# ScalarE takes the first MLP's eviction, and block inverses and reads from DRAM get places in the weight stream

## The chip, the cores and the metric

One core of a Trainium2 chip runs the whole program. The metric is the device time of one execution in microseconds (us), the median of several runs. TensorE (PE) multiplies, VectorE (DVE) and ScalarE (ACT) do element-wise work, and SyncE (SP) issues the DMAs, in order, one queue. Every engine works through its own list of instructions in order.

## The reference, cut to what matters

Two blocks in a chain, on 256 tokens (272 with 16 meta tokens in the first block's mixer) of width 2048, all in float32. The first has attention, an S5 state space mixer and a squared-ReLU MLP; the second has three branches (Hyena, HGRN2, gated DeltaNet) and an MLP of its own. The lines that the change touches:

```python
def first_block(...):
    ...
    h2 = _rmsnorm(h_res, norm_mlp_g[l])
    h_res = h_res + jnp.square(jax.nn.relu(h2 @ w_up[l])) @ w_down[l]     # 2048 -> 8192 -> 2048

def _delta_scan(q, k, v, g, beta, s0):          # once on the context, once on x, both directions
    ...
    a = eye + jnp.where(strict, jnp.einsum('bhtk,bhsk->bhts', kb, kc) * decay, 0.0)
    sol = lax.linalg.triangular_solve(a, rhs, left_side=True, lower=True, unit_diagonal=False)
    ...

def forget(fz, lb):                              # HGRN2: log forget gate lf and key kk
    f = lb + (1.0 - lb) * jax.nn.sigmoid(fz)
    return heads(jnp.log(jnp.maximum(f, HG_F_MIN))), heads((1.0 - lb) * jax.nn.sigmoid(-fz))
```

The context runs through DeltaNet and HGRN2 too, for their states alone. `mod_c` and `mod` (adaLN) are products of a vector with `w_ada`.

## The kernel before, in words

**The stream.** 1016 pieces of weights, 128 x 1024 floats (512 KB) each, go one by one through the same steps (`load_w`, L326): SP issues the DMA into `w` (4 buffers), ACT copies it rounded to `wh` (L334), DVE subtracts what is left over into `wl` (L335; 3 buffers each), and PE makes three products from it, with the input split the same way: wh·xh, wh·xl (or wl·xh) and wl·xh. `linear` (L355 to L357) has the weights move past 128 tokens at a time, 512 columns wide; `linear_t` (L390 to L392) has the weights stand and 256 tokens move past. This text counts places in the stream by pieces.

**Accumulators.** PSUM has three of them (tag `a`). A pass of `linear_t` uses two and has 8 matmuls of each kind to a piece, first all for one accumulator, then all for the other.

**The first MLP** (`mlp`, L977) takes pieces 153 to 408: four groups of 32 pieces up (8 passes of 4) and 32 down. Each pass up gives two tiles `ps` (128 x 256). DVE evicts one with max(ps, 0)·rstd in one instruction (L988, recorded as L541, the helper `stt`) into `r` (2 buffers), ACT squares it (L989), ACT copies it rounded (L402) and DVE subtracts (L403): the input of the way down. The second MLP, on pieces near the end, has no rstd to multiply by, and ACT evicts there (L986).

**Work beside the stream.** The order of everything is set when the program is built, by a scheduler that takes instructions by priority bands: stores to and loads from DRAM by the helper `dma` first, then what belongs to a weight piece, then other work, then the products. `tc.issue_after(ins)` holds an instruction back until behind `ins` on the same engine; it is an order, not a semaphore. Beside the first MLP run `ada_steps` (L436: one 128 x 1024 product with the vector `cb` on DVE, L460, for every few pieces), then `delta_context` (L1378: two halves of 4 heads) and `gla_context`. From piece 409 on the second block's input products are spilled to DRAM in the order dk, dq, dv, ab, dz, hq, ff, fb, hi, hg, hy (`spill_t`, `spill_i`), and `delta_x`, `gla_x` and the Hyena branch read them back and work beside the stream.

**DeltaNet** (`delta_heads`, L1252 on): `conv_silu` (L1105) reads a spilled tile and makes a short convolution; `l2n` (L1118) squares it on ACT (L1124) and sums over channels on PE (L1125); `delta_gates` (L1137) has four small transposes (L1161); `block_inverse` (L1182) inverts 32 x 32 triangles, 31 steps of a product (L1201, recorded as L538, tile `T4c`) and a sum (L1202, `T4a`) on DVE, of t x t elements at step t; then PE merges blocks.

**HGRN2** (`gla_x`): DVE and ACT make the log gates `E` and keys `qE` for 4 heads, SP writes them to DRAM (`xlf` L1507, `xkk` L1508) and reads them back for each head (recorded as L250, the helper `dma`, into `Bh`), and PE turns each head's log gates (L1529).

Of the kernel before, what the change touches and what calls it, by code (L numbers as in the profile page):

```python
# [208 lines left out]
def emit(tc, I, out, vat, cat):  # L209
# [169 lines left out]
    def linear_t(xh, xl, W, ci, n, evict, mid=None):  # L379
# [4 lines left out]
        for kb in range(nkb):  # L384
            for i, h, l in load_w(W[ci, kb]):
                for c in range(2):
                    for j in range(4):
                        k = kb * 8 + i * 4 + j
                        s = slice(j * 256 + c * 128, j * 256 + (c + 1) * 128)
                        T.matmul(acc[c], h[:, s], xh[k][:, 0:n], start=(k == 0), stop=False)  # L390
                        T.matmul(acc[c], h[:, s], xl[k][:, 0:n], start=False, stop=False)  # L391
                        T.matmul(acc[c], l[:, s], xh[k][:, 0:n], start=False, stop=(k == nk - 1))  # L392
# [43 lines left out]
    def ada_steps(p, row, dst, j0, n):  # L436
# [371 lines left out]
    def spill_ab(xT, dst):  # L808
        ps = psum("a", [32, NT])
        with band(0):  # L810
# [5 lines left out]
            tt(l[:, :512], w[:, :512], h[:, :512].bitcast(F32), ALU.subtract)  # L816
        with band(2):
            for k in range(16):
                sl = slice(k * 32, k * 32 + 32)
                T.matmul(ps, h[:, sl], xT[0][k][:, 0:NT], start=(k == 0), stop=False)  # L820
# [182 lines left out]
    wa_p[0] = es_wa.enter_context(tc.tile_pool(name="wa", bufs=2))  # L1003
    ride(ada_steps(ada_p, 0, mod, 32, 48), RATES[0])
# [100 lines left out]
    def conv_silu(p, o, src, r0, wname, wcol, row):  # L1105
# [4 lines left out]
        ts(o, a, w[1], ALU.mult)  # L1110
# [7 lines left out]
    def l2n(p, pk, xs, scales):  # L1118
# [18 lines left out]
    def delta_gates(p, pk, src):  # L1137
# [22 lines left out]
        for c in range(2):  # L1160
            T.transpose(ps[:, c, 0], e[:, c * 128:(c + 1) * 128], ident[:32, :32])  # L1161
            T.transpose(ps[:, c, 1], be[:, c * 128:(c + 1) * 128], ident[:32, :32])
# [19 lines left out]
    def block_inverse(p, MX, XT, KD):  # L1182
# [69 lines left out]
    def delta_heads(p, pk, src, h0, nh, gates, row, S_in, S_out, tb):  # L1252
# [5 lines left out]
        kT = [conv_silu(pk, tb([128, NT], f"kT{j}"), src["dk"], (j0 + j) * 128, "dck", j0 + j, row) for j in range(nk)]  # L1258
        qT = [conv_silu(pk, tb([128, NT], f"qT{j}"), src["dq"], (j0 + j) * 128, "dcq", j0 + j, row)
              for j in range(nk if full else 0)]  # L1260
        l2n(p, pk, kT + qT, [1.0] * nk + [128.0 ** -0.5] * len(qT))
# [52 lines left out]
        block_inverse(p, MX, XT, KD)  # L1314
# [63 lines left out]
    def delta_context():  # L1378
# [11 lines left out]
        for half in range(2):  # L1390
            delta_heads(p, p2_, cd, half * 4, 4, gates, NT, None, S0d, tb)
# [12 lines left out]
    xd["hi"] = scratch("xhi", [NT, 1024])  # L1404
    spill_t("w2_dk", uT, xd["dk"], mid=lambda: turn_u(3))
# [51 lines left out]
    def delta_x():  # L1457
# [3 lines left out]
        gates = delta_gates(eg.enter_context(tc.tile_pool(name="dg", bufs=1)), dk_p, xd["ab"])  # L1461
# [16 lines left out]
        o, last = delta_heads(p, p2_, xd, 0, 8, gates, 64, S0d, None, tb)  # L1478
# [5 lines left out]
    def gla_x():  # L1484
# [29 lines left out]
        for h in range(8):  # L1514
# [7 lines left out]
            for d in range(2):  # L1522
# [5 lines left out]
                for t in range(2):  # L1528
                    T.transpose(ps[:, t], lf[:, t * 128:(t + 1) * 128], ident)  # L1529
# [430 lines left out]
```

## Time and profile before

| | before |
|---|---|
| runs, median of 3 | 3569.97 us |
| lowest and highest run | 3565.4 and 3572.29 us |
| profiled execution, its own time | 3558.18 us |
| its span | 3556.4 us |
| granted TensorE clock, mean | 0.986 |
| DVE busy | 2472.0 us (70%) |
| ACT busy | 1868.0 us (53%) |

The span is the stretch from the first to the last instruction that the profile shows, 1.8 us shorter than that execution's own time. Busy shares are means over the whole program; a stage of 80 us with a full engine can't be seen in them. "A <- B: total, times, longest" in the view of waits means that an instruction of A stood idle until B was done.

### The profile page before, as it was taken

The page shows a single profiled execution, that of the slowest core. Times are in us where ns is not written, and L with a number is a line of the kernel's source. Part 1 is how long each engine was busy: PE and PEld are TensorE (multiplying, and loading weights), DVE is VectorE, ACT ScalarE, POOL GpSimd, SP SyncE. Part 2 cuts the span into 40 slices and gives each one's busy share as a digit, 9 for nine tenths or more (in the row PEclk, how much of TensorE's full clock was granted, in tenths as well). Part 3 has the DMA queues.
Part 4 walks back from the last instruction along what each step waited for, and adds up shares of the span by engine and source line. Part 5 has one row for each costly group of instructions (what it writes and reads, how often), then busy time and mean ns, then how long its engine had stood idle before and what let it go on. Part 6 is the DMA issues. An engine that isn't in the chain of part 4 may idle for free.

```text
span 3556.4 us, 60034 instructions
## 1 busy us (share of the span) xinstructions
PE 3454.9 (97%) x23748; PEld 2981.6 (84%) x23748; DVE 2472.0 (70%) x3806; ACT 1868.0 (53%) x2936; POOL 2.6 (0%) x13
## 2 busy tenths in 40 slices
PE   7999999999999999999999999999999999999998
PEld 5567899887888989888898889887887798989897
DVE  6778756696968767656946898848855755555557
ACT  5568746545456534445456666545444454545453
POOL 0000000000000000000000000000000000000000
PEclk9999999999999999999999999999999999999999
DMA  7754465665667888765648645565566567666655
GB/s 243 263 183 128 150 216 190 185 206 180 216 204 261 273 287 279 249 203 156 190 125 265 191 123 164 173 189 171 168 191 211 180 220 226 218 220 223 213 191 173
DMA packets 262772, 719.94 MB, mean 202 GB/s; under 512 B 51229, under 2 KB 96453, under 8 KB 261445
## 3 DMA queue, kind: packets, MB, share of 16 engines
q1 hardware_dynamic: 262490, 716.10, 62.9%
q8 instruction: 186, 3.05, 0.3%
q14 instruction: 96, 0.79, 0.1%
HBM read 684.98 MB, written 31.01 MB: 201 GB/s over the span
## 4 chain that ended last, share of the span: by engine, by line
PE 48%; DVE 4%; DMA 2%; ACT 1%; issue 1%; SPq 0%; DVEq 0%; ACTq 0%
PE ps L357 8%; PE ps L356 8%; PE ps L355 8%; PE ps L392 6%; PE ps L391 6%; PE ps L390 6%; DVE wl L335 1%; ACT wh L334 1%; PE ps L1547 0%; DMA xlf<-E 0%; DVE T4c L538 0%; PE ps L1586 0%; PE ps L1709 0%; PE ps L1654 0%; PE ps L1599 0%
## 5 line engine op out<-in xcount | busy, mean ns | idle before, releaser
L335 DVE TENSOR_TENSOR wl<-w,wh 128x1024 fp32r<-128x1024 f32 x1016 | 1239.1, 1221 | 760.7 <-ACT wh L334 756.8
L334 ACT ACTIVATE wh<-w 128x1024 fp32r<-128x1024 f32 x1016 | 1075.2, 1059 | 1129.0 <-PE ps L357 619.7
L390 PE MATMUL ps<-Ah,wh 128*128 128x256 f32 (+1 forms) x3904 | 1110.5, 285 | 15.1 <-DVE r L541 10.0
L392 PE MATMUL ps<-Ah,wl 128*128 128x256 f32 (+1 forms) x3904 | 1115.9, 286 | 9.4 <-DVE wl L335 9.2
L391 PE MATMUL ps<-Al,wh 128*128 128x256 f32 (+1 forms) x3904 | 1112.6, 285 | 0.0
L390 PEld LDWEIGHTS ps<-Ah,wh 128*128 128x128 f32 x3904 | 741.8, 190 | 30.4 <-DVE r L541 12.2
L392 PEld LDWEIGHTS ps<-Ah,wl 128*128 128x128 f32 x3904 | 741.7, 190 | 25.6 <-DVE wl L335 12.6
L391 PEld LDWEIGHTS ps<-Al,wh 128*128 128x128 f32 x3904 | 738.4, 189 | 9.4 <-issue 7.5
L357 PE MATMUL ps<-wh,Bl 128*128 128x512 f32 x1344 | 534.1, 397 | 0.0
L356 PE MATMUL ps<-wl,Bh 128*128 128x512 f32 x1344 | 528.9, 394 | 2.5 <-DVE wl L335 2.5
L355 PE MATMUL ps<-wh,Bh 128*128 128x512 f32 x1344 | 529.4, 394 | 1.3 <-DVE r L541 1.0
L356 PEld LDWEIGHTS ps<-wl,Bh 128*128 128x128 f32 x1344 | 252.8, 188 | 63.9 <-DVE wl L335 5.3
L356 PE MATMUL ps<-wl,Ah 128*128 128x512 f32 x752 | 301.2, 400 | 0.0
L355 PE MATMUL ps<-wh,Ah 128*128 128x512 f32 x752 | 299.8, 399 | 0.4 <-ACT stg L1797 0.4
L357 PE MATMUL ps<-wh,Al 128*128 128x512 f32 x752 | 299.8, 399 | 0.0
L355 PEld LDWEIGHTS ps<-wh,Bh 128*128 128x128 f32 x1344 | 253.2, 188 | 55.1 <-DVE r L541 1.4
L357 PEld LDWEIGHTS ps<-wh,Bl 128*128 128x128 f32 x1344 | 252.5, 188 | 55.1 <-issue 0.8
L356 PEld LDWEIGHTS ps<-wl,Ah 128*128 128x128 f32 x752 | 140.4, 187 | 38.4 <-issue 7.4
L357 PEld LDWEIGHTS ps<-wh,Al 128*128 128x128 f32 x752 | 140.5, 187 | 36.5 <-issue 5.4
L355 PEld LDWEIGHTS ps<-wh,Ah 128*128 128x128 f32 x752 | 140.6, 187 | 35.7 <-issue 3.7
L460 DVE SCALAR_TENSOR_TENSOR wa<-wa,cb 128x1024 f32<-128x1024 f32 x96 | 116.9, 1217 | 5.0 <-ACT cb L446 5.0
L989 ACT ACTIVATE r<-r 128x256 f32<-128x256 f32 x128 | 53.0, 415 | 75.7 <-DVE r L541 73.7
(581 smaller groups left out, 3374.2 us busy)
## 6 DMA issues: line engine op xcount, KB each, us to landing
w<-in_w_ff_dram SPq DMA_DIRECT2D x288, 512.0 KB, 4.8
w<-in_w_up_dram SPq DMA_DIRECT2D x128, 512.0 KB, 5.2
w<-in_w_down_dram SPq DMA_DIRECT2D x128, 512.0 KB, 5.2
w<-in_w_ada_dram SPq DMA_DIRECT2D x96, 512.0 KB, 4.6
wa<-in_w_ada_dram SPq DMA_DIRECT2D x96, 512.0 KB, 5.8
w<-in_w_gate_dram SPq DMA_DIRECT2D x96, 512.0 KB, 4.2
w<-in_w_out_dram SPq DMA_DIRECT2D x64, 512.0 KB, 4.3
w<-in_w_hy_dram SPq DMA_DIRECT2D x48, 512.0 KB, 4.3
```

The costliest lines, as they stand in the source:

```text
L334: A.activation(out=h, in_=w, func=AF.Copy)
L335: pace[1] = V.tensor_tensor(out=l, in0=w, in1=h.bitcast(F32), op=ALU.subtract)
L355: T.matmul(acc[t], xh[k][:, lo:hi], hs, start=(k == 0), stop=False)
L356: T.matmul(acc[t], xh[k][:, lo:hi], ls, start=False, stop=False)
L357: T.matmul(acc[t], xl[k][:, lo:hi], hs, start=False, stop=(k == nk - 1))
L390: T.matmul(acc[c], h[:, s], xh[k][:, 0:n], start=(k == 0), stop=False)
L391: T.matmul(acc[c], h[:, s], xl[k][:, 0:n], start=False, stop=False)
L392: T.matmul(acc[c], l[:, s], xh[k][:, 0:n], start=False, stop=(k == nk - 1))
L460: V.scalar_tensor_tensor(out=w, in0=w, scalar=1.0, in1=cb, op0=ALU.mult, op1=ALU.mult, accum_out=part[:, j, i:i + 1])
L989: A.activation(out=r, in_=r, func=AF.Square)
```

## The change

1. **Eviction.** In the first MLP ACT now takes max(ps, 0) out of PSUM and DVE multiplies the result in SBUF by rstd (`tt(r, r, scale)`); square, copy and subtraction follow as they did. That is 64 ACT instructions more; DVE has 64 multiplications in place of 64 evictions.
2. **Block inverses.** A `Pacer` holds each of the 62 operations of a block inverse behind the subtraction `wl` of a given weight piece: it starts at piece k, gives each piece a budget, and an operation of step t costs 60 + t². The context's halves begin at pieces m0 + 15 and m0 + 85 with budget 800 (m0 = 153, the first MLP's start), that of x at m1 + 62 with 1250 (m1 = 409, the start of the spills).
3. **Work on x that reads DRAM.** The first operation of eight `conv_silu` is held behind the subtractions of pieces m1 + 9 to m1 + 22, the matmuls of `l2n` behind the first product of piece m1 + 23, the gates' transposes behind that of m1 + 46, and the log gates' transposes of the first HGRN2 head behind that of m1 + 108.
4. **Second `cb`.** In `ada_steps` the second half of the vector is loaded three pieces ahead of its use.

Nothing else is added or taken away; PE, DVE and SP have as many instructions of each kind as before, but for the 64 of point 1.

```diff
+    subs, prods = [], []
+    class Pacer:
+        def __init__(self, k, per):
+            self.k, self.per, self.left = k, per, per
+        def __call__(self, cost):
+            if self.left < cost and self.left < self.per:
+                self.k, self.left = self.k + 1, self.per
+            self.left -= cost
+            return tc.issue_after(subs[min(self.k, len(subs) - 1)].ins)
...
                 pace[1] = V.tensor_tensor(out=l, in0=w, in1=h.bitcast(F32), op=ALU.subtract)
+                subs.append(pace[1])
...
             for j in range(2):
...
-                T.matmul(acc[t], xh[k][:, lo:hi], hs, start=(k == 0), stop=False)
+                mm = T.matmul(acc[t], xh[k][:, lo:hi], hs, start=(k == 0), stop=False)
+                if t == 0 and j == 0:
+                    prods.append(mm)
...
         for at, (i, j) in enumerate(steps):
+            own = wa_p[0] is not None
             if j == 0:
+                if i and own:
+                    yield
                 cb = tl(p, [128, 1024], "cb")
-                nc.sync.dma_start(cb, I["cvec"][row, i * 1024:(i + 1) * 1024].partition_broadcast(128))
+                with ExitStack() as es:
+                    if i and own:
+                        es.enter_context(tc.issue_after(pace[0].ins))
+                    nc.sync.dma_start(cb, I["cvec"][row, i * 1024:(i + 1) * 1024].partition_broadcast(128))
                 A.activation(out=cb, in_=cb, func=AF.Silu)
-            own = wa_p[0] is not None
+                if i and own:
+                    yield
+                    yield
...
             def ev(j, ps):
                 r = tl(mw_p, [128, NT], "r")
-                if scale is None:
-                    A.activation(out=r, in_=ps, func=AF.Relu)
-                else:
-                    stt(r, ps, 0.0, scale, ALU.max, ALU.mult)
+                A.activation(out=r, in_=ps, func=AF.Relu)
+                if scale is not None:
+                    tt(r, r, scale, ALU.mult)
                 A.activation(out=r, in_=r, func=AF.Square)
...
+    def place(seq, k):
+        return ExitStack() if k is None else tc.issue_after(seq[k].ins)
...
-        ts(o, a, w[1], ALU.mult)
+        with place(subs, at):
+            ts(o, a, w[1], ALU.mult)
...
-            T.matmul(ps, C("onecol", 7 - j, 7 - j + n), sq, start=(j == 0), stop=(j == n - 1))
+            with place(prods, at):
+                T.matmul(ps, C("onecol", 7 - j, 7 - j + n), sq, start=(j == 0), stop=(j == n - 1))
...
         for t in range(1, 32):
-            tt(tm[:, 0:t, 0:t], X[:, 0:t, 0:t], U[:, 0:t, t].unsqueeze(1).to_broadcast([P, t, t]), ALU.mult)
-            V.tensor_reduce(out=X[:, 0:t, t], in_=tm[:, 0:t, 0:t], axis=AX.X, op=ALU.add, negate=True)
+            with pacer(60 + t * t):
+                tt(tm[:, 0:t, 0:t], X[:, 0:t, 0:t], U[:, 0:t, t].unsqueeze(1).to_broadcast([P, t, t]), ALU.mult)
+            with pacer(60 + t * t):
+                V.tensor_reduce(out=X[:, 0:t, t], in_=tm[:, 0:t, 0:t], axis=AX.X, op=ALU.add, negate=True)
...
-            delta_heads(p, p2_, cd, half * 4, 4, gates, NT, None, S0d, tb)
+            delta_heads(p, p2_, cd, half * 4, 4, gates, NT, None, S0d, tb, Pacer(m0 + 15 + 70 * half, 800))
...
-        o, last = delta_heads(p, p2_, xd, 0, 8, gates, 64, S0d, None, tb)
+        o, last = delta_heads(p, p2_, xd, 0, 8, gates, 64, S0d, None, tb, Pacer(m1 + 62, 1250), m1)
...
-                for t in range(2):
-                    T.transpose(ps[:, t], lf[:, t * 128:(t + 1) * 128], ident)
+                with place(prods, m1 + 108 if h == 0 else None):
+                    for t in range(2):
+                        T.transpose(ps[:, t], lf[:, t * 128:(t + 1) * 128], ident)
```

**DVE in the first MLP**, steps 27 to 29 of the context's first block inverse (`T4c`, `T4a`: the inverse; `wl`: the stream; `r`: the eviction or its product; `Bl`: the hidden tile's subtraction; `wa`: adaLN; `x`: a product of the way down being added). Before:

```order
L538 TENSOR_TENSOR T4c_14446<-T4a_14445,T4b_14444 64x27x27
L1202 TENSOR_REDUCE T4a_14445<-T4c_14446 64x27
L541 SCALAR_TENSOR_TENSOR r_8048<-ps_7923,rsb_7051 128x256
L335 TENSOR_TENSOR wl_8097<-w_8094,wh_8096 128x1024
L403 TENSOR_TENSOR Bl_8052<-r_8048,Bh_8051 128x256
L541 SCALAR_TENSOR_TENSOR r_8055<-ps_7924,rsb_7051 128x256
L460 SCALAR_TENSOR_TENSOR wa_7931,adap_7233<-wa_7931,cb_7234 128x1024
L403 TENSOR_TENSOR Bl_8059<-r_8055,Bh_8058 128x256
L335 TENSOR_TENSOR wl_8130<-w_8127,wh_8129 128x1024
L538 TENSOR_TENSOR T4c_14446<-T4a_14445,T4b_14444 64x28x28
L335 TENSOR_TENSOR wl_8160<-w_8157,wh_8159 128x1024
L1202 TENSOR_REDUCE T4a_14445<-T4c_14446 64x28
```

With the change, steps 27 and 28:

```order
L565 TENSOR_TENSOR T4c_14510<-T4a_14509,T4b_14508 64x27x27
L1241 TENSOR_REDUCE T4a_14509<-T4c_14510 64x27
L348 TENSOR_TENSOR wl_8430<-w_8427,wh_8429 128x1024
L565 TENSOR_TENSOR T4c_14510<-T4a_14509,T4b_14508 64x28x28
L348 TENSOR_TENSOR wl_8448<-w_8445,wh_8447 128x1024
L487 SCALAR_TENSOR_TENSOR wa_8348,adap_7235<-wa_8348,cb_7236 128x1024
L1241 TENSOR_REDUCE T4a_14509<-T4c_14510 64x28
L348 TENSOR_TENSOR wl_8469<-w_8466,wh_8468 128x1024
```

The first inverse, at pieces 166 to 191 before, is at 169 to 207; the second, 210 to 240 before, at 240 to 278. One of the last steps has two pieces to itself now. The first two ways up are pieces 153 to 184 and 217 to 248, the ways down 185 to 216 and 249 to 280. The inverse for x, 469 to 487 before, is at 472 to 497.

**The same engine, an eviction's product** under the first inverse, with the change (its ACT part stands at the place in the stream where DVE's eviction stood):

```order
L348 TENSOR_TENSOR wl_7973<-w_7970,wh_7972 128x1024
L565 TENSOR_TENSOR r_7919<-r_7919,rsb_7051 128x256
L565 TENSOR_TENSOR T4c_14510<-T4a_14509,T4b_14508 64x19x19
L348 TENSOR_TENSOR wl_8003<-w_8000,wh_8002 128x1024
L421 TENSOR_TENSOR Bl_7924<-r_7919,Bh_7923 128x256
L565 TENSOR_TENSOR r_7927<-r_7927,rsb_7051 128x256
```

The product stands right behind a `wl`, and one step of the inverse behind it.

**SP, where `gla_x` writes its gates and reads the first heads back** (`E` and `qE`: log gates and keys; `Bh`: a head read back; `xfb`, `xhi`: spills). Before:

```order
L1508 DMA xkk_22395<-qE_22404 128x4x256
L796 DMA xfb_15536<-stg_18695 128x256
L331 DMA w_18793<-in_w_hi_dram 128x1024
L250 DMA Bh_22499<-xkk_22395 128x256
L250 DMA Bh_22787<-xkk_22395 128x256
L796 DMA xfb_15536<-stg_18698 128x256
L331 DMA w_18811<-in_w_hi_dram 128x1024
L1507 DMA xlf_22393<-E_22403 128x4x256
L331 DMA w_18823<-in_w_hi_dram 128x1024
L331 DMA w_18855<-in_w_hi_dram 128x1024
L250 DMA Bh_22498<-xlf_22393 128x256
```

With the change:

```order
L1549 DMA xlf_22457<-E_22467 128x4x256
L344 DMA w_19161<-in_w_hg_dram 128x1024
L1550 DMA xkk_22459<-qE_22468 128x4x256
L250 DMA Bh_22562<-xlf_22457 128x256
L250 DMA Bh_22850<-xlf_22457 128x256
L832 DMA xhi_15604<-stg_19063 128x512
L250 DMA Bh_22563<-xkk_22459 128x256
L250 DMA Bh_22851<-xkk_22459 128x256
L832 DMA xhi_15604<-stg_19066 128x512
L344 DMA w_19199<-in_w_hg_dram 128x1024
```

The log gates go out and come back first now, and stand 12 pieces later in the stream; the keys follow. PE's transposes of them stand 11 to 12 pieces later, those of the other direction 17. The matmuls of `l2n` for x stand 4 to 5 pieces later on PE, the gates' transposes 4, the merge and the states of `delta_x` 11. Hyena's first two chunks stand 13 to 17 pieces later, its third and fourth where they stood.

## Rows read from the trace of the kernel before

**Rows 1.** The page's first part: busy time, share of the span, instructions.

```profile
PE 3454.9 (97%) x23748; PEld 2981.6 (84%) x23748; DVE 2472.0 (70%) x3806; ACT 1868.0 (53%) x2936; POOL 2.6 (0%) x13
```

**Rows 2.** Waits of PE, whole span: what for, us in total, times, longest.

```profile
PE ps L1529 <- DMA Bh<-xlf: 5.1, 1, 5.1
PE ps L1125 <- ACT cin L1124: 4.5, 1, 4.5
...
PE ps L1547 <- ACT seg L1513: 1.8, 1, 1.8
```

**Rows 3.** Waits of PE, 690 to 1550 us (the first MLP).

```profile
PE ps L390 <- DVE r L541: 10.0, 9, 1.7
PE ps L356 <- DVE wl L335: 1.7, 4, 0.6
...
PE ps L392 <- DVE wl L335: 1.4, 3, 0.7
```

**Rows 4.** Waits of PE, 1550 to 1580 us (the first row), 1716 to 1786 us (the second).

```profile
PE ps L392 <- DVE wl L335: 1.5, 1, 1.5
...
PE ps L392 <- DVE wl L335: 5.8, 8, 1.6
```

**Rows 5.** Stretches: length, busy PE PEld DVE ACT POOL (count), clock, DMA share, GB/s.

```profile
717.00:801.00 84.00, 78.36 (x594) 73.85 (x593) 82.62 (x127) 37.72 (x55) 0.00 (x0) 1.00 0.62 205
897.00:990.00 93.00, 87.03 (x665) 82.37 (x664) 89.84 (x125) 38.79 (x53) 0.00 (x0) 1.00 0.67 208
1350.00:1400.00 50.00, 50.00 (x425) 50.00 (x424) 37.34 (x53) 24.23 (x34) 0.00 (x0) 1.00 0.88 274
...
1567.00:1574.00 7.00, 4.49 (x14) 2.34 (x15) 4.07 (x7) 2.28 (x6) 0.00 (x0) 0.51 0.54 170
1716.00:1786.00 70.00, 64.20 (x521) 61.81 (x520) 67.87 (x95) 29.67 (x41) 0.00 (x0) 1.00 0.64 200
1918.00:1926.00 8.00, 6.37 (x17) 5.17 (x18) 2.89 (x6) 3.13 (x5) 0.00 (x0) 0.57 0.95 310
```

**Rows 6.** Tile T4c on DVE, 717 to 801 us: count, ns min/median/max, first and last start.

```profile
L538 DVE TENSOR_TENSOR T4c<-T4a,T4b x31: 145/625/1966, 721.0 to 796.6; 64x1 f32<-64x1 f32 x1, 64x4 f32<-64x4 f32 x1, 64x9 f32<-64x9 f32 x1, 64x16 f32<-64x16 f32 x1
```

**Rows 7.** Groups by line and form: busy, mean ns | idle before, ended by.

```profile
L335 DVE TENSOR_TENSOR wl<-w,wh 128x1024 fp32r<-128x1024 f32 x1016 | 1239.1, 1221 | 760.7 <-ACT wh L334 756.8 <-PE ps L392 0.9 <-issue 0.2
...
L334 ACT ACTIVATE wh<-w 128x1024 fp32r<-128x1024 f32 x1016 | 1075.2, 1059 | 1129.0 <-PE ps L357 619.7 <-PE ps L391 414.3 <-issue 32.1
...
L460 DVE SCALAR_TENSOR_TENSOR wa<-wa,cb 128x1024 f32<-128x1024 f32 x96 | 116.9, 1217 | 5.0 <-ACT cb L446 5.0
L989 ACT ACTIVATE r<-r 128x256 f32<-128x256 f32 x128 | 53.0, 415 | 75.7 <-DVE r L541 73.7
...
L541 DVE SCALAR_TENSOR_TENSOR r<-ps,rsb 128x256 f32<-128x256 f32 x64 | 26.6, 416 | 4.8 <-PE ps L392 4.8
L986 ACT ACTIVATE r<-ps 128x256 f32<-128x256 f32 x64 | 23.9, 373 | 14.3 <-PE ps L392 14.3
```

**Rows 8.** The chain that ended last, 1550 to 1580 us: start, us, what.

```profile
1558.82 2.40 DMA xdq<-stg
...
1561.24 5.05 DMA cin<-xdq
```

**Rows 9.** The same chain, 1895 to 1925 us.

```profile
1899.05 9.26 DMA xkk<-qE
...
1910.35 6.31 DMA xlf<-E
...
1916.72 2.78 DMA Bh<-xlf
```

**Rows 10.** DVE's instructions in order of time, 1895 to 1925 us.

```profile
1904.24 2.36 DVE L538 TENSOR_TENSOR E<-E,x 128x1024 f32<-128x1024 f32 x2
```

**Rows 11.** Busy time on tile T4c alone (columns of rows 5), the two operations of an inverse.

```profile
720.90:800.80 79.90, 39.50 (x62) 1.00 0.63 208
...
1721.00:1781.20 60.20, 39.90 (x62) 1.00 0.63 202
```

More of the change, by code (lines that the diff above doesn't have):

```diff
@@ L389, in linear_t @@
                         s = slice(j * 256 + c * 128, j * 256 + (c + 1) * 128)
-                        T.matmul(acc[c], h[:, s], xh[k][:, 0:n], start=(k == 0), stop=False)
+                        mm = T.matmul(acc[c], h[:, s], xh[k][:, 0:n], start=(k == 0), stop=False)
+                        if c == 0 and j == 0:
+                            prods.append(mm)
                         T.matmul(acc[c], h[:, s], xl[k][:, 0:n], start=False, stop=False)
@@ L815, in spill_ab @@
             A.activation(out=h[:, :512], in_=w[:, :512], func=AF.Copy)
-            tt(l[:, :512], w[:, :512], h[:, :512].bitcast(F32), ALU.subtract)
+            subs.append(V.tensor_tensor(out=l[:, :512], in0=w[:, :512], in1=h[:, :512].bitcast(F32),
+                                        op=ALU.subtract))
         with band(2):
@@ L819, in spill_ab @@
                 sl = slice(k * 32, k * 32 + 32)
-                T.matmul(ps, h[:, sl], xT[0][k][:, 0:NT], start=(k == 0), stop=False)
+                mm = T.matmul(ps, h[:, sl], xT[0][k][:, 0:NT], start=(k == 0), stop=False)
+                if k == 0:
+                    prods.append(mm)
                 T.matmul(ps, h[:, sl], xT[1][k][:, 0:NT], start=False, stop=False)
@@ L1003, in emit @@
     wa_p[0] = es_wa.enter_context(tc.tile_pool(name="wa", bufs=2))
+    m0 = len(subs)
     ride(ada_steps(ada_p, 0, mod, 32, 48), RATES[0])
@@ L1102, in gla_context, with conv_silu @@
         es.close()
-    def conv_silu(p, o, src, r0, wname, wcol, row):
+    def place(seq, k):
+        return ExitStack() if k is None else tc.issue_after(seq[k].ins)
+    def conv_silu(p, o, src, r0, wname, wcol, row, at=None):
         a = tl(p, [128, NT], "cin")
@@ L1116, in conv_silu, with l2n @@
         return o
-    def l2n(p, pk, xs, scales):
+    def l2n(p, pk, xs, scales, at=None):
         n = len(xs)
@@ L1135, in l2n, with delta_gates @@
                 stt(a, a, scales[j], ps, ALU.mult, ALU.mult)
-    def delta_gates(p, pk, src):
+    def delta_gates(p, pk, src, at=None):
         ab = tl(p, [32, NT], "ab")
@@ L1159, in delta_gates @@
         ps = psum("tp", [128, 2, 2, 32])
-        for c in range(2):
-            T.transpose(ps[:, c, 0], e[:, c * 128:(c + 1) * 128], ident[:32, :32])
-            T.transpose(ps[:, c, 1], be[:, c * 128:(c + 1) * 128], ident[:32, :32])
+        with place(prods, at):
+            for c in range(2):
+                T.transpose(ps[:, c, 0], e[:, c * 128:(c + 1) * 128], ident[:32, :32])
+                T.transpose(ps[:, c, 1], be[:, c * 128:(c + 1) * 128], ident[:32, :32])
         A.activation(out=gb, in_=ps, func=AF.Copy)
@@ L1180, in delta_gates, with block_inverse @@
         return g, b, ec, nec, bs
-    def block_inverse(p, MX, XT, KD):
+    def block_inverse(p, MX, XT, KD, pacer):
         P = 8 * KD
@@ L1250, in merge_blocks, with delta_heads @@
                             A.activation(out=XT[q, ks, xc], in_=ps[q], func=AF.Copy, scale=-1.0)
-    def delta_heads(p, pk, src, h0, nh, gates, row, S_in, S_out, tb):
+    def delta_heads(p, pk, src, h0, nh, gates, row, S_in, S_out, tb, pacer, at=None):
         g, be, ec, nec, bs = gates
@@ L1257, in delta_heads @@
         j0 = h0 // 2
-        kT = [conv_silu(pk, tb([128, NT], f"kT{j}"), src["dk"], (j0 + j) * 128, "dck", j0 + j, row) for j in range(nk)]
-        qT = [conv_silu(pk, tb([128, NT], f"qT{j}"), src["dq"], (j0 + j) * 128, "dcq", j0 + j, row)
+        ats = [None] * 9 if at is None else [at + k for k in (9, 9, 13, 13, 17, 17, 22, 22, 23)]
+        kT = [conv_silu(pk, tb([128, NT], f"kT{j}"), src["dk"], (j0 + j) * 128, "dck", j0 + j, row, ats[j])
+              for j in range(nk)]
+        qT = [conv_silu(pk, tb([128, NT], f"qT{j}"), src["dq"], (j0 + j) * 128, "dcq", j0 + j, row, ats[4 + j])
               for j in range(nk if full else 0)]
-        l2n(p, pk, kT + qT, [1.0] * nk + [128.0 ** -0.5] * len(qT))
+        l2n(p, pk, kT + qT, [1.0] * nk + [128.0 ** -0.5] * len(qT), ats[8])
         gr = []
@@ L1313, in delta_heads @@
             A.activation(out=v[h], in_=ps, func=AF.Copy)
-        block_inverse(p, MX, XT, KD)
+        block_inverse(p, MX, XT, KD, pacer)
         merge_blocks(p, MX, XT, KD)
@@ L1404, in emit @@
     xd["hi"] = scratch("xhi", [NT, 1024])
+    m1 = len(subs)
     spill_t("w2_dk", uT, xd["dk"], mid=lambda: turn_u(3))
@@ L1460, in delta_x @@
         eg = ExitStack()
-        gates = delta_gates(eg.enter_context(tc.tile_pool(name="dg", bufs=1)), dk_p, xd["ab"])
+        gates = delta_gates(eg.enter_context(tc.tile_pool(name="dg", bufs=1)), dk_p, xd["ab"], m1 + 46)
         eg.close()
```

## The prediction, on record before the changed kernel ran

> **What bounds the kernel now.** First the page's busy times: PE works 3454.9 of 3556.4 us [rows 1], so the whole of what a better order can give is the 101 us in which PE does nothing, and what it loses at a low clock. The stream never stops for long; it is held up in places. So the second view is the waits of PE. Each group names the instruction that stood idle and what it waited for: one matmul of a later stage waits 4.5 us for the squares of `l2n`, one transpose 5.1 us for log gates from DRAM, one 1.8 us for `seg` [rows 2]. In the first MLP nine first products wait 10.0 us in all for `r`, that is for an accumulator that DVE has not evicted, and seven matmuls 3.1 us for `wl` [rows 3]. Beside the inverse for x it is 5.8 us, all for `wl` [rows 4].
>
> Why DVE is late is in the third view, the stretches. Over the program it is 70% busy, but 82.62 of 84 us and 89.84 of 93 us beside the context's inverses and 67.87 of 70 us beside that of x [rows 5]: full. PE has 5.6, 6.0 and 5.8 us idle there. In a stretch without side work PE is busy throughout, with 425 matmuls in 50 us; at 24 to a piece of `linear_t` that is 17.7 pieces, **2.82 us a piece** [rows 5]. That is what DVE is given for each piece.
>
> Two stretches show a second loss: 1567 to 1574 and 1918 to 1926 us ran at a granted clock of 0.51 and 0.57 [rows 5], nearly the lower of the two levels (1.2 of 2.4 GHz), each beside a wait of 4 to 5 us [rows 2].
>
> **Step 1, the eviction.** ACT gets 64 instructions more. The second MLP has the same one: 373 ns, and there ACT waits for PE, not PE for ACT [rows 7]. That is 64 × 0.373 = 24 us on an engine that is half idle; I cost it at nothing, for the 11.3 us of a pass up (4 pieces) hold 4 × 1.059 for `wh` and 2 × (0.373 + 0.415 + a copy like the square, 0.415), together 6.6 us. Without that cover it is up to 24 us. DVE's multiplication has no row; nearest is the eviction that it replaces, of the same size, 416 ns [rows 7]. Below that a gain from leaving PSUM isn't excluded, above it 64 × 0.1 us or so; I take no difference. What the step gives is a way out of DVE's list: the accumulator is free when ACT has read it, and only the hidden tile waits for DVE; the way down needs it pieces later.
>
> A rule speaks against this. The row first: 416 ns on DVE, 373 on ACT for the same 128 x 256 floats out of PSUM [rows 7]. The Trainium skill (ScalarE: Activation LUTs, Rules for kernel authors) says that `relu`, `max` and `mul` belong on VectorE, not ScalarE. By that rule alone the first MLP would give nothing, and the sum below would be 19.8 us instead of 29.4, or 3550; by the rows the instruction itself is no dearer, and here DVE is the full engine. What the rule could do at worst is rival C.
>
> **Step 2, the context's inverses.** Work is only moved. The two operations of an inverse take 39.5 us [rows 11], with single ones up to 1.97 us [rows 6], in which time no `wl` and no eviction is made. The first inverse runs at pieces 166 to 191, 25 pieces in 79.9 us, so 3.2 us a piece. DVE's other work is (82.62 − 39.5) us over 84/3.2 = 26 pieces [rows 5, 11], 1.65 us each. Before: 25 × 1.65 + 39.5 = 81 us of work for 25 × 2.82 = 70 us. With the change, over 38 pieces: 102 us for 107. The second (as long, 30 pieces, some 1.6 us of other work) goes from 88 for 85 to 100 for 107, and most of it out of a way up. So DVE has room, but only 5 to 7%.
>
> Of the 10.0 + 1.7 + 1.4 = 13.1 us in rows 3, I let 3.5 stay: a quarter, because order within a piece still matters in a list so full, and because `gla_context`, 42 to 44 pieces later, now lies under a denser adaLN. **Gain 9.6 us**; ends 0 and 13.1. Its own lateness costs nothing: it is done near piece 331, and nothing asks for it before piece 409.
>
> **Step 4, `cb`,** is inside that sum: the one time that DVE waits for it, 5.0 us [rows 7], the eviction behind it is late, and that is the longest of the nine waits, 1.7 us [rows 3]. Load and activation are as many as before, three pieces earlier than needed.
>
> **Step 3, DeltaNet on x.** The spilled tile takes 2.40 us into DRAM and 5.05 us back [rows 8]; DVE stands before the first short convolution meanwhile, with a `wl` in its list behind it, and PE stands before `l2n`. Now DVE reaches it some 2 to 4 pieces later and PE 4 to 5 pieces, 11 to 14 us, which is more than the 7.5 us of both transfers. Gone: 4.5 us [rows 2] and 1.5 us for `wl` [rows 4]; and with the idle time, I take it, the low clock: 4.49 us of work at 0.51 took 2.2 us too long [rows 5]. **Gain 8.2 us**; ends 2 and 8.2.
>
> The inverse for x goes from 18 pieces (60.2 us) to 25. Its other work is (67.87 − 39.9) us over 70/3.34 = 21 pieces [rows 5, 11], 1.33 us. Before: 64 us for 51. After: 73 for 70.5, still 3 us too much, about a `wl` buffer's worth. Of the 5.8 us I leave 1.5. **Gain 4.3 us**; ends 0 and 5.8.
>
> **Step 3, HGRN2 on x.** DVE's last product of the gates starts at 1904.24 and lasts 2.36 us [rows 10], so they are ready at 1906.6, but SP issues their write at 1910.35: it stood 9.26 us before reads of keys that weren't in DRAM yet [rows 9]. Then 6.31 and 2.78 us [rows 9] to PE. With the log gates first the write can go at once: 3.7 us off the wait of 5.1. Gates and transposes move by 11 to 12 pieces alike, so nothing else is gained there. If 1.4 us stay, the clock shouldn't fall: 6.37 us at 0.57 cost 2.7 [rows 5]. `seg` comes through the same queue; half of its 1.8 us [rows 2]. **Gain 7.3 us**; ends 0 and 9.6. The Hyena chunks that are pushed 13 to 17 pieces back catch up by the third, so their end costs nothing; if they did not, branch products would wait.
>
> **The sum.** −9.6 − 8.2 − 4.3 − 7.3 = −29.4 us. The profiled execution took 3558.18 us, so 3528.8 by its measure. The runs shown lie 7 to 14 us above it; the same off their median, 3569.97, is **3540.6 us**. All upper ends together give 36.7, and I allow 10 us for small waits beside the named ones: 3523 from the median, 3518 from the lowest run, 3565.4. All lower ends: 2 us, 3568.
>
> **Rivals.** *A: DVE stays the bound.* The wait for `r` becomes one for `wl`, as it is already for x [rows 4]. For it: 95% busy by my own count and 104% for x. Against it: before, the excess was 4 to 25% and cost only 6 us a stage. Then steps 1 and 2 and the inverse give 2 us, HGRN2 nothing while the reads stay as slow, and DeltaNet its 8.2: 3560.
>
> *B: SP starves the stream.* With the change three reads that wait for writes follow each other with no new piece between. They would hold SP 6.31 us for the log gates and up to 9.26 for the keys [rows 9], while four buffers hold 11.3 us of weights, part of which is still coming in. If each direction costs 4 us, HGRN2's 7.3 is gone and 0.7 more: 3541 + 8 = 3549.
>
> *C: slower, ACT becomes the late engine.* ACT's square must wait for DVE's product, and `wh` of the next piece stands behind it in ACT's list. Before, the square already waited 73.7 us for DVE [rows 7]. A pass has 11.3 − 6.6 = 4.7 us of room, so it decides at 2.3 us of waiting for each of two tiles. Behind a long inverse step and two `wl` (1.97 + 2 × 1.22 = 4.4 us [rows 6, 7]) it would be 2 × 4.4 − 4.7 = 4.1 us a pass over; 14 passes beside inverses or other full DVE work make 57 us: 3541 + 57 = 3598. Against it: in the order the product stands right behind a `wl`, with the inverse's step behind it. The rule of the Trainium skill above points this way.
>
> *D: the waits only move.* PE gets faster to the next thing that is late: the merges of blocks, whose loads from DRAM are unchanged, and Hyena. What is saved is waited for there: 3568.
>
> **How the numbers follow.** Forecast 0.57 (3526 to 3553), A 0.17, B 0.11, D 0.08, C 0.07. The measurement can tell about 0.2%, 7.1 us: faster means under 3562.8. The forecast, B and most of A are there, 0.82; a part of A and D are the same, 0.11; C is slower, 0.07. The range goes from 3518 to 3564: nearly all of the forecast, B and A, some 0.83.
>
> **What would show it.** In the profile after: PE's wait for an accumulator in the first MLP under 3 us; DVE 95% or less beside the context's inverses; the waits of 4.5 and 5.1 us gone or under 2, with no granted clock near 0.5 beside `l2n` and the first log gates; PE busy about as long as before, idle some 75 us. Wrong: `wl` or `wh` among PE's waits with over 10 us in the first MLP (A or C), a `w` from DRAM before PE near the first head (B), new waits of PE in the merges or in Hyena (D).

## The result, and the profile after

The changed kernel takes 3534.7 us (median of 4 runs, 3532.59 to 3535.75) where the kernel before takes 3569.95 (4 runs, 3565.4 to 3572.29): a ratio of 0.9903, 95% interval 0.9888 to 0.9918, so 35 us less. Forecast were 29.4 us less and 3541 us. The 45 runs of the kernel before that were made beside the experiments have medians of 3565.3 us; against those the change would be 30.6 us less.

The two profiled executions differ by less, 3558.18 to 3535.75 us, since that of before is quicker than each of its four runs, and that of after is the slowest of its four. Most of what follows compares stretches of the stream: from the start of one piece's `wl` to that of another's, at the same pieces in every trace. The view of stretches for PE, before, cut at pieces 156, 348, 408 and 660 (length, PE busy, clock, DMA share, GB/s):

```profile
0.00:685.40 685.40, 657.02 (x4264) 0.99 0.60 196
685.40:1328.10 642.70, 622.38 (x4183) 0.98 0.71 229
1500.50:2505.30 1004.80, 971.93 (x8217) 0.98 0.57 178
2505.30:3535.50 1030.20, 1020.05 (x5941) 0.99 0.64 205
```

The same with the change:

```profile
0.00:689.50 689.50, 657.70 (x4264) 0.99 0.59 195
689.50:1316.50 627.00, 617.70 (x4183) 0.98 0.72 233
1489.70:2480.30 990.60, 963.35 (x8210) 0.98 0.58 180
2480.30:3512.90 1032.60, 1021.20 (x5940) 0.99 0.64 205
```

The first MLP (second line) gives 15.7 us for the same 4183 matmuls, the work beside the second block's products (third line) 14.2. Ahead and behind, where nothing is changed, the trace after is 4.1 and 2.4 us longer, and between the second and the third line, in the last pieces of the first MLP, 0.8 (172.4 to 173.2). Of the 4.1 us, 3.5 are waits of the start, which were 2.6 us before:

```profile
PE ps L508 <- DMA w<-in_w_ada_dram: 6.1, 9, 1.2
```

So in these two stretches it is 29.9 us: the sum that I forecast, but shared out among the steps otherwise than I had it.

Line numbers have moved: with the change L348 makes `wl` (before: L335), L369 to L373 and L406 to L410 are the products (L355 to L357, L390 to L392), L1161 and L1198 the matmuls of `l2n` and the gates' transposes (L1125, L1161), L1572 the log gates' transposes (L1529) and L1590 their products with `seg` (L1547); some experiments have them 4 or 5 lines further on, or a few back.

PE's waits between 690 and 1550 us, after, against 10.0 and 3.1 us [rows 3]:

```profile
PE ps L406 <- ACT r L1015: 3.2, 3, 2.0
...
PE ps L372 <- DVE wl L348: 0.4, 1, 0.4
PE ps L410 <- DVE wl L348: 0.3, 1, 0.3
```

Stretches beside the three inverses, after (columns of rows 5; first the same 84 us as there, then the first, the second and that of x with the change):

```profile
717.00:801.00 84.00, 84.00 (x645) 80.91 (x644) 74.53 (x125) 45.75 (x72) 0.00 (x0) 1.00 0.71 234
735.00:840.00 105.00, 105.00 (x664) 94.84 (x663) 97.91 (x135) 49.49 (x67) 0.00 (x0) 1.00 0.69 227
968.00:1076.00 108.00, 107.58 (x592) 92.90 (x591) 104.28 (x140) 46.69 (x58) 0.00 (x0) 1.00 0.76 248
1696.00:1776.00 80.00, 77.53 (x643) 76.14 (x643) 71.15 (x94) 34.73 (x45) 0.00 (x0) 1.00 0.69 221
```

PE isn't idle at all in 84 and 105 us now and for 0.4 of 108; DVE is 93 and 97% busy, near the 95 and 93% worked out. So beside the context's inverses a DVE as full as that cost PE 0.4 us.

Between 1490 and 2300 us the wait of `l2n` is gone. Those of HGRN2 are not:

```profile
PE ps L1572 <- DMA Bh<-xlf: 5.0, 2, 3.1
PE ps L1590 <- ACT seg L1555: 4.0, 1, 4.0
```

### The profile page after: what moved, and what is told of

Read it like the earlier page. It is cut to its first block, busy times and chain, and to the rows that moved or that the text cites. A ratio compares the mean times of both kernels' runs of the same rounds, so it can differ in the third digit from the quotient of the medians.

```text
span 3533.9 us, 60120 instructions
## 1 busy us (share of the span) xinstructions
PE 3445.0 (97%) x23748; PEld 2977.9 (84%) x23748; DVE 2466.8 (70%) x3806; ACT 1880.8 (53%) x2995; POOL 2.6 (0%) x13
## 4 chain that ended last, share of the span: by engine, by line
PE 84%; DMA 6%; DVE 5%; ACT 3%; issue 2%; SPq 0%; DVEq 0%; ACTq 0%
PE ps L373 13%; PE ps L372 13%; PE ps L369 13%; PE ps L410 11%; PE ps L409 11%; PE ps L406 11%; DVE wl L348 2%; DMA w<-in_w_ada_dram 2%; ACT wh L347 1%; PE ps L720 1%; PE ps L508 1%; PE ps L1278 1%; PE ps L701 1%; PE ps L1280 1%; PE ps L1380 0%
## 5 line engine op out<-in xcount | busy, mean ns | idle before, releaser
L348 DVE TENSOR_TENSOR wl<-w,wh 128x1024 fp32r<-128x1024 f32 x1016 | 1239.8, 1221 | 765.3 <-ACT wh L347 757.7
L410 PE MATMUL ps<-Ah,wl 128*128 128x256 f32 (+1 forms) x3904 | 1113.9, 286 | 3.1 <-DVE wl L348 2.7
L406 PE MATMUL ps<-Ah,wh 128*128 128x256 f32 (+1 forms) x3904 | 1109.1, 284 | 7.5 <-ACT wh L347 4.3
L406 PEld LDWEIGHTS ps<-Ah,wh 128*128 128x128 f32 x3904 | 741.6, 190 | 20.9 <-issue 10.3
L410 PEld LDWEIGHTS ps<-Ah,wl 128*128 128x128 f32 x3904 | 742.0, 190 | 16.6 <-issue 10.1
L373 PE MATMUL ps<-wh,Bl 128*128 128x512 f32 x1344 | 533.9, 397 | 0.0
L369 PE MATMUL ps<-wh,Bh 128*128 128x512 f32 x1344 | 530.3, 395 | 1.1 <-ACT wh L347 1.1
L369 PE MATMUL ps<-wh,Ah 128*128 128x512 f32 x752 | 300.7, 400 | 0.4 <-ACT stg L1840 0.4
L373 PE MATMUL ps<-wh,Al 128*128 128x512 f32 x752 | 300.0, 399 | 0.0
L369 PEld LDWEIGHTS ps<-wh,Bh 128*128 128x128 f32 x1344 | 253.7, 189 | 54.7 <-ACT wh L347 1.4
L373 PEld LDWEIGHTS ps<-wh,Bl 128*128 128x128 f32 x1344 | 253.0, 188 | 54.9 <-issue 0.6
L373 PEld LDWEIGHTS ps<-wh,Al 128*128 128x128 f32 x752 | 140.2, 186 | 35.9 <-issue 5.4
L369 PEld LDWEIGHTS ps<-wh,Ah 128*128 128x128 f32 x752 | 140.3, 187 | 35.4 <-issue 3.7
L487 DVE SCALAR_TENSOR_TENSOR w<-w,cb 128x1024 f32<-128x1024 f32 x32 | 39.2, 1225 | 50.3 <-DMA w<-in_w_ada_dram 50.3
```

Source lines behind the costliest of these rows:

```text
L369: mm = T.matmul(acc[t], xh[k][:, lo:hi], hs, start=(k == 0), stop=False)
L406: mm = T.matmul(acc[c], h[:, s], xh[k][:, 0:n], start=(k == 0), stop=False)
L487: V.scalar_tensor_tensor(out=w, in0=w, scalar=1.0, in1=cb, op0=ALU.mult, op1=ALU.mult, accum_out=part[:, j, i:i + 1])
```

## The experiments

Times are medians; all ratios are to runs of the kernel before on the same chip (medians 3565.25 to 3565.32 us), as recorded; the quotient of the two medians differs from them by up to 0.0011. The change's own ratio is 0.9903, to 3569.95 us. Two stretches are given for each: **M**, pieces 156 to 348 (642.7 us before, 627.0 with the change), and **X**, pieces 408 to 660 (1004.8 and 990.6). An identical part of the program differs by some 10 us between traces: the first 156 pieces take from 685.3 to 695.1 us, from the program's start, in these kernels, all of which have the same work there. So a stretch tells more of a part than a median does. But each is from one execution, and it varies too: seven kernels with the change's first MLP have an M of 626.8 to 629.7 us, the kernel before and run 4, which share theirs, 642.7 and 645.9, and four kernels with the change's work on x (the change, runs 1, 3 and 4) an X of 990.6, 988.4, 987.7 and 988.6. A difference of under 3 us tells nothing, and the change's X is the longest of its four. The executions profiled of runs 8, 9, 11 and 12 are the slowest of their kernels, that of run 5 is the quickest.

**1. Eviction back on DVE**, all else as in the change.

```diff
-                A.activation(out=r, in_=ps, func=AF.Relu)
-                if scale is not None:
-                    tt(r, r, scale, ALU.mult)
+                if scale is None:
+                    A.activation(out=r, in_=ps, func=AF.Relu)
+                else:
+                    stt(r, ps, 0.0, scale, ALU.max, ALU.mult)
```

> The change with DVE's one-instruction eviction put back in the first MLP; all else stays. The two traces give the change 15.7 us between the pieces 156 and 336 (685.4 to 1295.0 us before, 689.5 to 1283.4 after) and 13.4 us between 408 and 660. Theory S (both parts share the first gain, since both take work out of DVE's full list): about 6 us are lost, 3541 us, and waits for the accumulator (r) come back with 3 to 6 us in the first MLP. Rival E (the eviction is the whole of it, the inverses' places do nothing there): 15 us lost, 3550. Rival P (the places are the whole of it): 3535, the same as the change.

Measured: 3534.07 us, 0.9917 (0.9904 to 0.9931); M 630.5, X 988.4. The waits for the accumulator stay away:

```profile
PE ps L406 <- DVE r L568: 1.5, 4, 0.5
```

That is rival P within what can be told; the theory's 6 us are not there in the time, and M has 3.5. They are not waits: PE is idle for 8.9 us of M here and for 9.3 with the change.

**2. The eviction alone**, on the kernel before (the `r` lines of experiment 1's diff the other way round).

> The kernel before with ScalarE's eviction alone; no places, the second cb as before. Theory S: 6 to 8 us faster than before, 3562 to 3564, with PE's waits in the first MLP turned from r into wl. Rival E: 15 us faster, 3555. Rival P: 3570, no change. If ACT became a late engine by this alone, as a rival of the prediction had it: slower than before, PE waiting for r or wh from ACT.

Measured: 3558.29 us, 0.9991 (0.9979 to 1.0003), so no change to be told, though the interval and the medians, which are 7.0 us apart, don't exclude theory S. M speaks against it: 643.3, between the 642.7 and 645.9 of the first MLP as before. PE's waits in the first MLP:

```profile
PE ps L414 <- DVE wl L352: 9.6, 10, 1.8
PE ps L376 <- DVE wl L352: 2.2, 6, 0.6
```

The 10.0 us for `r` [rows 3] have become 9.6 for `wl`: DVE is as late as it was, and PE meets it at its next instruction. That is the wait of the prediction's rival A, to the letter, but in this kernel, not in the change.

**3. The context's inverses without their places** (`NoPacer` holds nothing back).

```diff
-            delta_heads(p, p2_, cd, half * 4, 4, gates, NT, None, S0d, tb, Pacer(m0 + 15 + 70 * half, 800))
+            delta_heads(p, p2_, cd, half * 4, 4, gates, NT, None, S0d, tb, NoPacer())
```

> The change without the places of the context's two inverses; eviction, second cb and everything on x stay. Theory S: 8 us slower than the change, 3543, with DVE full again beside the inverses and PE waiting for wl there. Rival E: 3535, as the change. Rival P: 15 us slower, 3550.

Measured: 3545.57 us, 0.995 (0.9936 to 0.9964), outside the change's interval; M 638.5, so 11.5 of the 15.7 us are gone, and the waits are those of run 2:

```profile
PE ps L414 <- DVE wl L352: 9.3, 9, 1.8
PE ps L376 <- DVE wl L352: 1.8, 5, 0.6
```

By time and by M the run lies between theory S (8 us) and rival P (15). Run 8 below has the places without ACT's eviction and an M of 630.8, 11.9 us under that of before. So the places give most of the first MLP's gain, by leaving them out and by having them alone. No run tells the spreading from the new position: the second inverse has also moved from beside a way up to mostly beside a way down.

**4. The places on x alone**, first MLP as before (eviction, context's inverses and `cb` undone).

> The kernel before with the places on x alone (inverse, short convolutions, l2n, gates, first log gates); the first MLP with its eviction, inverses and cb as before. If the gain on x stands by itself: 13 us faster than before, 3557, and pieces 408 to 660 take 991 us instead of 1005. Rival: what is saved there is only there because the first MLP delivers in another order: 3570.

Measured: 3551.59 us, 0.9965 (0.9952 to 0.9978); X 988.6, M 645.9. The gain on x stands by itself: 13.7 us between the medians where 13 were expected.

**5. No place for the first log gates.**

```diff
-                with place(prods, m1 + 108 if h == 0 else None):
+                with place(prods, None):
```

> The change without the place of the first log gates' transposes (all else stays). Theory N (the gain forecast for HGRN2, 7.3 us, did not come: the wait there is 5.0 us after as 5.1 before): 3531 to 3538, and pieces 408 to 660 take 988 to 993 us as with the change. Rival (the place holds off a longer wait that the earlier inverse would otherwise make): 3542 or more, with over 5 us of waiting before the first log gates.

Measured: 3536.33 us, 0.9922 (0.9904 to 0.994); X 984.8. Theory N: the place gives nothing. X is 5.8 us shorter without it than with the change, 2.9 than the shortest of its four.

**6. The inverse for x without places.**

```diff
-        o, last = delta_heads(p, p2_, xd, 0, 8, gates, 64, S0d, None, tb, Pacer(m1 + 62, 1250), m1)
+        o, last = delta_heads(p, p2_, xd, 0, 8, gates, 64, S0d, None, tb, NoPacer(), m1)
```

> The change without the places of the inverse for x. By the prediction the inverse is worth 4.3 us: 3539, with 5 to 6 us of waits for wl back beside it. Rival (spreading is worth more than the waits it removes, as on the context): 10 us or more, 3545.

Measured: 3530.33 us, 0.9909 (0.9891 to 0.9927); X 992.9, 2.3 more than the change and 5.2 more than the shortest of its four. The waits for `wl` are back, 5.8 us as in [rows 4], and the time shows nothing of them:

```profile
PE ps L414 <- DVE wl L352: 5.8, 9, 1.5
PE ps L1576 <- DMA Bh<-xlf: 5.3, 1, 5.3
```

Neither the forecast 3539 nor the rival's 3545. In this kernel PE waits longer beside the inverse, but not for `seg` as long as in the change (2.0 against 4.0 us).

**7. No place for any read from DRAM** (convolutions, `l2n`, gates, log gates; the two diffs below and that of run 5).

> The change without any place for work that reads DRAM (short convolutions, l2n, gates, log gates); eviction, cb and all inverses' places stay. By the prediction l2n's wait, the wl behind it and the low clock are worth 8.2 us: 3543, with the wait of 4 to 5 us and a granted clock near 0.5 back after 1550 us. Rival (PE would be held up at the next late thing anyway): 3535.

Measured: 3549.76 us, 0.9962 (0.9949 to 0.9975); X 1004.3, all that X had gained. PE's waits between 1490 and 2300 us have `l2n` and the gates back:

```profile
PE ps L1161 <- ACT cin L1159: 4.4, 1, 4.4
...
PE ps L1198 <- DVE dge L562: 1.5, 1, 1.5
```

The loss is nearly twice the 8.2 us of my sum; runs 10 and 12 divide it.

**8. The three inverses' places alone** (runs 7 and 1 together, and the second `cb` as before).

> The places of the three inverses alone: DVE's eviction, no places for reads, the second cb as before. Theory P (places are the whole gain of the first MLP, the eviction and cb give nothing): as the run without places for reads, within 4 us, 3539 to 3547. Rival (eviction and cb give the 3.4 us that two traces differ by between pieces 156 and 336, or more): 4 us or more above that run.

Measured: 3550.11 us, 0.9966 (0.9953 to 0.9978); M 630.8, X 1010.0. The time is that of run 7, as theory P says, though not in the 3539 to 3547 us that it named: eviction and `cb` are not to be seen in it. X is 5.7 us above run 7's, in the slowest of twelve executions.

**9. `seg` ahead of the gates**, and no place for the log gates.

```diff
+        seg = tl(pc, [128, 2, 896], "seg", F32R)
+        for d in range(2):
+            w = tl(p2_, [128, 4, NT], "E").rearrange("p l t -> p (l t)")
+            dma(w[:, :896], I["seg"][d])
+            A.activation(out=seg[:, d], in_=w[:, :896], func=AF.Copy)
         for i, hb in enumerate((0, 4)):
             nc.sync.dma_start(wide[i], heads_of(xd["hq"], hb, 4))
...
-        seg = tl(pc, [128, 2, 896], "seg", F32R)
-        for d in range(2):
-            w = tl(p2_, [128, 4, NT], "E").rearrange("p l t -> p (l t)")
-            dma(w[:, :896], I["seg"][d])
-            A.activation(out=seg[:, d], in_=w[:, :896], func=AF.Copy)
...
```

> The change without the place of the log gates' transposes, and with the two loads of seg and their copies put ahead of gla_x's gates instead of behind them. In the change seg waits 4.0 us: its buffer E is free only when the log gates written from it have landed (7.54 us), and then it takes 4.89 us itself; a low clock of 6.8 us follows. Theory: both go, some 4 + 3 us, 3528 to 3531, no wait for seg. Rival (the next late thing, the log gates of the first head, takes its place): 3535 with over 6 us of waits there.

Measured: 3530.92 us, 0.9899 (0.9885 to 0.9913); X 986.2. The wait for `seg` is gone, and another stands in its place:

```profile
PE ps L1590 <- ACT E L1592: 3.9, 3, 3.6
PE ps L1572 <- DMA Bh<-xlf: 1.7, 1, 1.7
```

The time is the one that the theory named, and the waits, 5.6 us, are nearly those of the rival. Against run 5, which has `seg` where it was, the intervals overlap and X is 1.4 us longer, so nothing is shown to be won. The time can't be told from the change's either.

**10. No place for the gates' transposes.**

```diff
-        gates = delta_gates(eg.enter_context(tc.tile_pool(name="dg", bufs=1)), dk_p, xd["ab"], m1 + 46)
+        gates = delta_gates(eg.enter_context(tc.tile_pool(name="dg", bufs=1)), dk_p, xd["ab"])
```

> The change without the place of the delta gates' four transposes; short convolutions and l2n keep theirs. Leaving out all places for reads cost 15 us, of which my sum names 8. Theory L (l2n is all of it, the rest is what its lateness brings after it): 3535 to 3538, no low clock between 1540 and 1700 us. Rival G (the gates are held up by themselves and bring the low clock of 13.7 us after 1640 us): 3541 to 3544, with that stretch back.

Measured: 3537.73 us, 0.9921 (0.9908 to 0.9933); X 996.6, 6.0 more than the change and 8.9 more than the shortest of its four. A low clock is back in 1620 to 1680 us, with only 2.2 us of idle PE (columns as in the first fence):

```profile
1620.00:1680.00 60.00, 57.77 (x358) 0.89 0.45 135
```

In the change the same 60 us have 1.00 and 427 matmuls:

```profile
1620.00:1680.00 60.00, 59.45 (x427) 1.00 0.54 166
```

The trace is rival G's, but the time is theory L's: 3 us between the medians, with overlapping intervals. And the place does not always keep the clock up: in three other kernels that have both places these 60 us have 0.97 (runs 3 and 6) and 0.94 (run 9).

**12. No place for convolutions and `l2n`.**

```diff
-        ats = [None] * 9 if at is None else [at + k for k in (9, 9, 13, 13, 17, 17, 22, 22, 23)]
+        ats = [None] * 9 if at is None else [None] * 9
```

> The change without the places of the short convolutions and of l2n; the gates' transposes keep theirs. Theory L: 3548 to 3551, with the wait of 4.5 us and low clocks after 1555 and after 1640 us. Rival G: 3543, with the low clock after 1555 alone.

Measured: 3545.53 us, 0.9943 (0.9931 to 0.9956); X 998.9, 8.3 more than the change. The interval lies apart from the change's. The wait of `l2n` is 4.7 us here, and the low clock comes after 1564 us and not after 1640: rival G, which named 3543. By X the two parts are 6.0 and 8.3, together 14.3, and run 7 has 13.7 for both with the log gates' place.

**11. Only what had shown a gain:** runs 1, 6 and 9 together.

> Only what has shown a gain: the places of the context's inverses, of the short convolutions, l2n and the gates, the second cb, and seg early; DVE's eviction is put back, the inverse for x and the log gates have no place. Theory (eviction, inverse for x and log gates' place give nothing): as the run with seg early, within 4 us. Rival (with two of them gone DVE is full again beside the inverse for x, since one covered for the other): 6 us or more above it, with waits for wl or r of over 8 us.

Measured: 3541.4 us (six runs, 3528.38 to 3547.04), 0.9924 (0.9908 to 0.9941); M 633.9, X 994.7. By X, in its slowest execution, it is 8.5 us above run 9, with these waits between 1490 and 2300 us:

```profile
PE ps L414 <- DVE wl L352: 6.4, 10, 1.5
PE ps L1595 <- ACT E L1597: 3.6, 1, 3.6
```

The lean version isn't better; the rival is nearer, though the runs spread too far to say by how much. No kernel here is clearly quicker than the change.

## Why the prediction was right, and where its steps were not

**What bounds the kernel** held, but idle time is only a little more than half of the gain: PE is idle 88.9 us instead of 101.5, not the 75 forecast, and its busy time, which I expected to stay, fell by 9.9 us for the same instructions. Of the 9.9, the low clock behind `l2n` and the gates (step 3 below) is a part; 4.7 are in M, where the mean clock is the same. Other signs missed too: the wait for an accumulator is 3.2 us and not under 3, DVE has 97% and not 95 beside the second inverse, and near the first log gates the wait stayed and the clock is still low (0.57 before [rows 5]):

```profile
1918.00:1926.00 8.00, 7.16 (x48) 7.19 (x49) 3.91 (x7) 3.40 (x6) 0.00 (x0) 0.79 0.71 208
```

**Step 1, the eviction: wrong as a cause.** I wrote that it gives "a way out of DVE's list". With DVE's eviction back, the time is the same (run 1), and alone it does nothing that M shows (run 2). Beside the context's places M leaves it 3 to 4 us, and not as idle time: the seven kernels with ACT's eviction have 626.8 to 629.7 there, the three with DVE's 630.5 to 633.9. What I should have seen: after the accumulator, the next instruction in PE's list needs a `wl`, from the same late engine. The prices were right: 374 ns for the activation, 417 for the product that has replaced 416 (the 0.1 us that I allowed above that was from no row). ACT's square, in the first line, waits for DVE less than it did:

```profile
L1018 ACT ACTIVATE r<-r 128x256 f32<-128x256 f32 x128 | 52.9, 414 | 31.2 <-DVE r L565 28.9
...
L1015 ACT ACTIVATE r<-ps 128x256 f32<-128x256 f32 x128 | 47.9, 374 | 26.8 <-PE ps L410 26.7
...
L565 DVE TENSOR_TENSOR r<-r,rsb 128x256 f32<-128x256 f32 x64 | 26.5, 417 | 0.3 <-ACT r L1015 0.3
```

The rule of the Trainium skill (ScalarE: Activation LUTs, Rules for kernel authors: `relu` and `max` on VectorE) is neither borne out nor contradicted by the times: run 1 has the eviction where the rule wants it, and its interval overlaps the change's. M speaks for ACT by 3.5 us. My 3550 by that rule was a misreading: it took the gain of the inverses' places away too, of which the rule says nothing.

**Step 2, the inverses' places: right in mechanism, too small.** Steps 1, 2 and 4 were to give 9.6 us together with at most 13.1; M gave 15.7, and runs 3 and 8 show 11.5 and 11.9 of them with the places. The waits that I summed, for `r` and `wl`, did as forecast: 13.1 us became 3.9, of which 3.2 are for ACT's eviction. The bound was too low because I summed only them: PE's idle time in M fell by 11.0 us, and its busy time by 4.7 for the same matmuls at the same mean clock (0.98). That part stands in no row of waits; where in M it was lost isn't shown. What of this the denser adaLN was to cost did not appear.

**Step 4, `cb`:** DVE's idle 5.0 us before `wa` [rows 7] is now 0.0:

```profile
L487 DVE SCALAR_TENSOR_TENSOR wa<-wa,cb 128x1024 f32<-128x1024 f32 x96 | 116.9, 1218 | 0.0
```

What it is worth stays open: runs 2 and 3, which differ in M by nothing else, have 643.3 and 638.5, but beside paced inverses runs 8 and 1 have 630.8 and 630.5.

**Step 3, DeltaNet's reads: right, but a part missing.** The wait, the `wl` and the low clock beside `l2n`, 8.2 us: run 12 has 8.3 by X. The gates' transposes, which I left at nothing, give 6.0 more by X (run 10), of which the medians show 3. I had their wait before me as small, but not what follows: in the kernel before, the matmuls of `l2n` and of the next steps bunch up behind it, PE is never idle, and yet the clock is low:

```profile
1655.00:1672.00 17.00, 17.00 (x69) 0.70 0.27 77
```

17 us at 0.70 are, as an estimate, 5.1 us too many. With the change 1540 to 1700 us have a clock of 1.00; that the place of the gates is the reason is likely by run 10, but not shown, as runs 3, 6 and 9 have it and a clock of 0.94 to 0.97 from 1620 to 1680.

**Step 3, the inverse for x:** forecast 4.3 us. The waits fell from 5.8 to 1.9 us, but the stretch X gives 2.3 (run 6) and the time nothing; run 11 against run 9, which also differ in the eviction, has 8.5. It stays open between 0 and 8.5.

**Step 3, HGRN2: wrong.** Forecast 7.3 us, nothing came (run 5: X is shorter without the place). The first transposes wait 3.1 us instead of 5.1, and those of the other direction 1.9 that they did not wait before: the 5.0 us in two times. The write did go out as soon as the gates were ready, as I said: the first direction's last product ends at 1908.69. That alone is worth 4.9 us and not 3.7, for before, too, the first of the two products was enough, and it ended at 1905.46 (I had read the end of both), while SP stood for 5.9 us of the 9.26 that I named, from 1902.40 to 1908.32. But now the gates were ready late. SP in the change, in order of time:

```profile
1893.77 1.74 SPq L250 DMA_DIRECT2D g<-xq  x4
...
1896.03 0.92 SPq L344 DMA_DIRECT2D w<-in_w_hi_dram  x2
...
1908.71 0.38 SPq L1549 DMA_DIRECT2D xlf<-E  x1
...
1914.52 1.08 SPq L250 DMA_DIRECT2D Bh<-xlf  x2
```

And the chain that ended last, from 1895 to 1925 and from 1960 to 1990 us:

```profile
1896.03 6.75 DMA w<-in_w_hi_dram
...
1972.68 7.54 DMA xlf<-E
1980.24 4.89 DMA E<-in_seg_dram
```

SP stood before reads of `xq` until 1893.77, the next weights went out at 1896.03 and took 6.75 us, `wl` waited for them, and the last products of the gates stand behind that `wl` on DVE. SP stood before these reads in the kernel before as well, from 1891.51 to 1895.40, but there the `wl` ahead of the gates' last products waited only 0.17 us; before and after:

```profile
1903.10 1.23 DVE L335 TENSOR_TENSOR wl<-w,wh 128x1024 fp32r<-128x1024 f32 x1 [0.17 <-ACT wh L334]
...
1903.98 1.23 DVE L348 TENSOR_TENSOR wl<-w,wh 128x1024 fp32r<-128x1024 f32 x1 [3.18 <-ACT wh L347]
```

From write to read it is 5.8 us, and the transpose follows 4.3 us later: together 10.1 us, where [rows 9] have 9.1. `seg`, which I thought to gain, waits 4.0 instead of 1.8 us, as its buffer is free only when log gates written from it have landed. This is rival B in a small form, as I read the two traces: SP's list sets when weights come, and weights when the gates are ready.

**Rival C**, ACT as the late engine, was to show in ACT's square: it waits 28.9 us for DVE's product where it was 73.7 for DVE's eviction [rows 7], and PE waits 3.2 us for ACT. Far from 57. **Rival D** did not come in the merges; in HGRN2 it is the 2.2 us more for `seg`.

That the sum was near (29.4 against 29.9 in the two stretches) was luck, for two errors met: M was forecast at 9.6 and gave 15.7, X at 19.8 and gave 14.2. The parts don't add up exactly, in X (8.3, 6.0 and 2.3, less 5.8 for the log gates' place, against 14.2) or in the times: places on x alone have 0.9965 and the change without reads 0.9962, together 26 of 35 us, with some 5 us of uncertainty on each.

## What to carry to other kernels

When an engine's list is full for a while, look for the block of work that fills it and spread that over more of the stream; taking one waiting instruction out of the list only moved PE's wait here to the next result of the same engine. After giving late work a place further back, look at what SP must read first: a queue that stands before a read also holds the weights, and through them the work that the read was waiting for. Beside a wait of PE, count the stretch of low clock that follows, also where PE is busy throughout, and compare stretches with equal work, for medians of a few runs hide parts under 5 us; take more than one trace of each, for here single stretches varied by 3 us.

## What the runs showed of the hardware that was not expected

The granted clock fell without idle time just before: in the kernel before PE was busy for all 9 us from 1650 to 1659 us, and yet from 1660 to 1669 us the clock was 0.50, its lower level, while PE made 21 matmuls, those of `l2n` and of the products of keys among them. Over the 17 us shown above it was 0.70, with 69 matmuls; the last wait, 1.3 us for the gates, lay ahead of 1650 us. And identical work at the program's start took from 685.3 us (run 6) to 695.1 (run 12), with 1.7 and 9.6 us of waits for `w_ada` from DRAM.
